# Two transformer layers with retrieved experts: all weighted v rows summed on VectorE, GpSimd left with the gathers, five row buffers instead of four

## The chip, the core and the metric

The kernel runs on one core of a Trainium2 chip. A core has TensorE (PE in the profile; its weight loads are PEld), VectorE (DVE), ScalarE (ACT), GpSimd (POOL) and SyncE (SP), each with its own instruction queue that it works off in order, and 16 DMA engines that move data between HBM and the on-chip memories. The metric is the device time of one execution in microseconds (us), as the median of several runs.

## The reference

The program is two layers of a diffusion backbone over 512 latent and 256 context tokens of width 1024. Each layer has attention (two kinds of heads, a projection before and after them, norms and gates) and then an expert retrieval, which is what the change touches:

```python
def chunk(xc):                       # 128 tokens
    q = (xc @ wq).reshape(PEER_CHUNK, PEER_HEADS, 2, PEER_DHALF)
    s = jnp.einsum('thpd,hpkd->thpk', q, sub_keys).astype(jnp.float32)
    sv, si = lax.top_k(s, PEER_TOPK)
    ...
    g = jax.nn.softmax(cv, axis=-1)
    u_sel = u[idx]                   # 128 experts for each token, rows of 1024
    v_sel = v[idx]
    a = jax.nn.gelu(jnp.einsum('td,thkd->thk', xc, u_sel).astype(jnp.float32), approximate=False)
    return jnp.einsum('thk,thkd->td', (g * a).astype(xc.dtype), v_sel)
```

Every token picks 8 x 16 = 128 of 16,384 experts. An expert is a row of u, whose product with the token gives a weight, and a row of v, which is added to the token's result with that weight. In the first layer this is done for two context tiles and four latent tiles of 128 tokens, in the second for the four latent tiles.

## The kernel before

**Two ways to the experts.** Five latent tiles (0, 1, 2 of layer 0 and 1, 2 of layer 1, `DENSE`) are *dense*: the whole table of a layer goes by once, 128 steps of 128 experts, and matrix products with all the tiles' tokens are made (`dense_experts`). Which experts count for a token is told by a weight array G, made earlier from one-hot products (`one_hots`, 32 groups of four tokens to a tile: "quads"). The five other tiles (both context tiles and latent tile 3 in layer 0, tiles 0 and 3 in layer 1) are *gathered* (`experts`): for each k of 0..127 one indirect DMA, issued by GpSimd, fetches one row per token (128 rows of 1024 float32, 512 KB) into a ring of four buffers `gv`. These five tiles are called jobs here; each has 128 u rows and then 128 v rows.

**What is done with a row.** A u row is multiplied with the tokens `btok` and summed along the row on VectorE (line 746). Of the v rows some go to VectorE, which multiplies by the token's weight and adds to accumulator 0 in one instruction (`scalar_tensor_tensor`, line 767); the others are scaled on ScalarE (line 763) and added to accumulator 1 by GpSimd (line 764). `SHARE` says who takes which by turns: half and half before the dense stream, two of three to VectorE during it. At a job's end VectorE adds the two accumulators (line 770). `LAG` = 3: the work on a row is issued behind the gather three rows later, so that rows are under way while older ones are worked on; a gather takes the buffer that the row four places earlier has left.

**Order.** Each layer begins with attention, routing, choice of experts and one-hots; there a scheduler (it simulates the program with its own idea of durations) places the instructions of each engine's queue. The gathered rows are woven in: 46% of them (353 of 768) in layer 0, 50% (256 of 512) in layer 1 (`AHEAD`). Then comes the dense stream, whose order is written by hand: a step's products and splits, and after them as many gathered rows as keep the pace even; in layer 1 only from step 16 on (`LATE`). 40 rows of layer 0 are left over for the beginning of layer 1 (`SPILL`).

**A dense step** e: the tables' tiles of step e + 1 (u) and e (v) are fetched by SP, each is split in two parts, of which ScalarE makes the leading one (line 870) and VectorE the rest (line 871); PE makes A (24 products, line 924); ScalarE applies GELU (927); VectorE multiplies by G (930); W is split as above (870, 871); PE adds the products of the step before (line 897, 18 in layer 0 and 12 in layer 1). So a step is 42 PE instructions in layer 0 and 36 in layer 1.

**One-hots.** Of the four one-hot products of a quad (`o2`), ScalarE makes one in two instructions (lines 850, 851), GpSimd one and VectorE two (line 854); VectorE also makes the other operand (842), PE multiplies (855) and ScalarE copies the result out (856).

Of the kernel before, what the change touches and what calls it, by code (L numbers as in the profile page):

```python
# [25 lines left out]
F32 = mybir.dt.float32  # L26
# [4 lines left out]
AF = mybir.ActivationFunctionType  # L31
# [3 lines left out]
D = 1024  # L35
# [15 lines left out]
# latent tiles whose experts run densely, per layer  # L51
# [6 lines left out]
ONPOOL = 1  # L58
O2B = 6
# of four tokens' one-hot products, those made on the scalar engine  # L60
ONACT = 1
ET = mybir.EngineType
MANUAL = {ET.PE, ET.DVE, ET.Activation, ET.Pool, ET.SP}
# who sums the v rows by turns: the vector engine, or the scalar engine and GpSimd
SHARE = ((0, 1), (0, 0, 1))
# rows on their way before the first is used
LAG = 3
# steps of the dense stream before it is joined by the rest of the gathered rows
LATE = (0, 16)
# gathered rows left for the next layer's beginning  # L70
SPILL = (40, 0)
# share of the gathered rows that goes ahead of the dense stream
AHEAD = (0.46, 0.5)
# float32 products of operands split exactly in two (0 the leading part), at float32 accuracy
# [5 lines left out]
# blocks of the pair list with one width: (offset, first a, number of a, width)  # L80
# [12 lines left out]
def body(ctx: ExitStack, tc: tile.TileContext, I, out):  # L93
# [6 lines left out]
    # pools of the phase at hand  # L100
# [17 lines left out]
    def gv_tile(n):  # L118
        return gat.tile([P, n], F32, tag="gv", name="gv", bufs=4)
# [14 lines left out]
    # column - row: key block before the query's may be seen where it is >= 0, the one after where <= 0  # L134
# [9 lines left out]
    # residual streams live in DRAM; hcur maps (stream, token tile) to the rows holding it now  # L144
# [23 lines left out]
    def big_w(src, cn):  # L168
        """rows of src in chunks of P, two to a tile -> [chunk] of [P, cn]."""
# [19 lines left out]
    def ada_w_early(after):  # L189
        """the same through the gather ring, which is idle before the first experts; starts once after is there."""  # L190
# [12 lines left out]
    def ada(l, m, early=None):  # L203
        """generator: appends to m the six vectors of both streams, two to a round, their four column blocks side by side."""
# [32 lines left out]
    def gate_row(t, l, i, st, n, q=nc.gpsimd):  # L237
        """t [p, 512 * x]: columns from n * 512 of gate i of the stream on every partition."""
        q.dma_start(t, gates[l, i][J[st]:J[st] + 1, n * 512:n * 512 + t.shape[1]].to_broadcast(list(t.shape)))
        return t  # L240

    def rstd_of(ss, n):
        """1 / sqrt(ss / n + eps), in place."""
# [919 lines left out]
```

## Times and profile before

| | us |
|---|---|
| runs | 4654.28, 4655.55, 4660.62 |
| median | 4655.55 |
| span of the profiled execution (first to last instruction) | 4664.8 |
| attention, routing and rows of layer 0 | 0 to 1452 |
| dense stream of layer 0 | 1452 to 2612 |
| beginning of layer 1 with 40 rows left over | 2612 to 2760 |
| attention, routing and rows of layer 1 | 2760 to 3700 |
| dense stream of layer 1 and the last rows | 3700 to 4665 |

For the profiled execution the page gives the span and no other time; it lies 9.25 us, or 0.2%, above the median of the runs. Within the stages the rows of job 0 are gathered from 348 to 1092 us, job 1 from 1104 to 1955, job 2 from 1963 to 2733, job 3 from 2970 to 3767 and job 4 from 3802 to 4638. A dense stream thus has *u stretches*, in which the rows at hand are u rows (1960 to 2345 and 3790 to 4220), and *v stretches* (1548 to 1960, 2345 to 2612, 4220 to 4640). The work of a dense step is the same in both.

### The profile page before, as it was taken

To read this page: it belongs to the slowest core of one execution; us is meant where nothing else is said; L and a number is where in the kernel's file an instruction comes from. 1 tells how busy PE (TensorE), PEld (TensorE's weight loads), DVE (VectorE), ACT (ScalarE), POOL (GpSimd) and SP (SyncE) were. 2 spreads that over 40 slices of the span, in tenths; PEclk is the share of its full clock that TensorE was granted. 3 is DMA by queue.
4 is the path that set the end of the run, shared out by engine and by line. 5 is a ranking of instruction groups with operands and counts; after the bars stand their busy time and mean duration, and the time that the engine had idled before them with its cause. 6 is when DMAs were issued, how large, how long until landed. Compare 5 with 4: busy or idle time off the path is not lost.

```text
span 4664.8 us, 59187 instructions
## 1 busy us (share of the span) xinstructions
PE 3753.1 (80%) x20350; PEld 3004.6 (64%) x20350; DVE 3507.7 (75%) x7582; ACT 1903.2 (41%) x3344; POOL 2473.8 (53%) x1818
## 2 busy tenths in 40 slices
PE   7886778597867999899999567678787688888786
PEld 2463457375756888788887445555576577776665
DVE  1256757978998888887788642767889988888887
ACT  2342334464634444333344444233465543334443
POOL 1114557685754577644466740254587744445665
PEclk9997889787988999999999889888798699999998
DMA  8578887677896988899988762788687789998887
GB/s 302 186 241 297 286 299 238 233 262 251 307 336 234 319 290 293 305 334 331 330 286 300 259 215 88 256 318 314 228 278 273 251 306 332 330 335 305 308 303 244
DMA packets 467487, 1306.55 MB, mean 280 GB/s; under 512 B 41569, under 2 KB 147809, under 8 KB 467185
## 3 DMA queue, kind: packets, MB, share of 16 engines
q0 software_dynamic: 199744, 726.26, 45.3%
q1 hardware_dynamic: 267440, 576.50, 35.5%
q8 instruction: 160, 2.62, 0.2%
q14 instruction: 143, 1.16, 0.1%
HBM read 1240.70 MB, written 61.90 MB: 279 GB/s over the span
## 4 chain that ended last, share of the span: by engine, by line
DVE 27%; issue 22%; PE 17%; DMA 16%; POOL 12%; ACT 6%; SPq 0%; POOLq 0%; ACTq 0%; DVEq 0%
POOL gv L742 9%; DMA gv<-u,idx 6%; DVE gv L746 5%; DVE vacc L767 5%; DMA gv<-v,idx 4%; POOL vacc L764 3%; PE m L632 3%; DVE v L871 3%; PE m L370 2%; ACT u L870 2%; PE m L506 2%; DVE o L854 2%; DMA raw<-uT 1%; DVE o L842 1%; DVE w L930 1%
## 5 line engine op out<-in xcount | busy, mean ns | idle before, releaser
L742 POOL DMA_INDIRECT gv<-u,idx x640 | 782.0, 1222 | 935.1 <-DVE a L746 590.8
L897 PE MATMUL o<-v,W 128*128 128x512 f32 x3840 | 973.2, 405 | 190.5 <-ACT W L870 166.4
L742 POOL DMA_INDIRECT gv<-v,idx x640 | 807.3, 1261 | 593.8 <-DVE vacc L767 318.9
L924 PE MATMUL A<-b,u 128*128 128x384 f32 (+1 forms) x6144 | 965.5, 313 | 51.5 <-ACT w L927 46.0
L924 PEld LDWEIGHTS A<-b,u 128*128 128x128 f32 x6144 | 933.2, 192 | 94.2 <-ACT w L927 73.2
L897 PEld LDWEIGHTS o<-v,W 128*128 128x128 f32 x3840 | 724.8, 193 | 379.6 <-ACT W L870 197.9
L746 DVE CUSTOM_DVE_ANT_0 gv<-gv,btok 128x1024 f32<-128x1024 f32 x640 | 766.5, 1220 | 142.7 <-DMA gv<-u,idx 141.3
L767 DVE SCALAR_TENSOR_TENSOR vacc<-gv,a,vacc 128x1024 f32<-128x1024 f32 x374 | 620.3, 1658 | 69.8 <-DMA gv<-v,idx 66.7
L764 POOL TENSOR_TENSOR vacc<-vacc,gv 128x1024 f32<-128x1024 f32 x256 | 621.6, 2428 | 79.8 <-ACT gv L763 75.6
L870 ACT ACTIVATE W<-w 128x384 fp32r<-128x384 f32 (+1 forms) x256 | 120.6, 471 | 1019.6 <-DVE w L930 1019.6
L871 DVE TENSOR_TENSOR u<-raw,u 128x1024 fp32r<-128x1024 f32 x256 | 340.8, 1331 | 131.6 <-ACT u L870 127.3
L763 ACT ACTIVATE gv<-gv,a 128x1024 f32<-128x1024 f32 x256 | 292.3, 1142 | 226.0 <-DMA gv<-v,idx 190.8
L370 PE MATMUL m<-w,aT 128*128 128x256 f32 (+3 forms) x704 | 261.1, 521 | 93.6 <-DMA w<-w_in 44.5
L871 DVE TENSOR_TENSOR W<-w,W 128x384 fp32r<-128x384 f32 (+1 forms) x256 | 208.5, 814 | 153.0 <-ACT W L870 153.0
L632 PE MATMUL m<-bT,wq 128*128 128x128 f32 x2560 | 319.4, 282 | 4.1 <-DMA wq<-wq 3.7
L871 DVE TENSOR_TENSOR v<-raw,v 128x1024 fp32r<-128x1024 f32 x256 | 313.7, 1226 | 5.5 <-ACT v L870 5.5
L632 PEld LDWEIGHTS m<-bT,wq 128*128 128x128 f32 x2560 | 306.5, 198 | 10.1 <-issue 3.7
L870 ACT ACTIVATE u<-raw 128x1024 fp32r<-128x1024 f32 x256 | 267.6, 1045 | 36.5 <-DMA raw<-uT 36.3
L370 PEld LDWEIGHTS m<-w,aT 128*128 128x128 f32 x704 | 145.7, 217 | 197.4 <-DMA w<-w_in 56.3
L870 ACT ACTIVATE v<-raw 128x1024 fp32r<-128x1024 f32 x256 | 267.4, 1045 | 7.9 <-PE o L897 7.7
L854 POOL TENSOR_SCALAR o<-io,i,gT 128x128 f32<-128x128 f32 x160 | 201.4, 1260 | 66.4 <-PE big L855 35.1
L506 PE MATMUL m<-dsu,pexp 128*128 128x128 f32 x1472 | 226.3, 299 | 6.0 <-ACT dsu L494 5.2
(215 smaller groups left out, 4923.0 us busy)
## 6 DMA issues: line engine op xcount, KB each, us to landing
raw<-uT SPq DMA_DIRECT2D x256, 512.0 KB, 5.8
raw<-v SPq DMA_DIRECT2D x256, 512.0 KB, 5.4
wq<-wq SPq DMA_DIRECT2D x144, 512.0 KB, 6.3
gv<-ada_w POOLq DMA_DIRECT2D x80, 512.0 KB, 5.6
Gd<-ar SPq DMA_DIRECT2D x80, 512.0 KB, 4.7
w<-w_out SPq DMA_DIRECT2D x72, 512.0 KB, 6.6
G<-Gd SPq DMA_DIRECT2D x16, 1536.0 KB, 13.9
G<-Gd SPq DMA_DIRECT2D x16, 1024.0 KB, 9.0
```

The source lines that it names most:

```text
L370: nc.tensor.matmul(ps[:, :cn], aT[:, k, :], w[k][:, :cn], start=(k == 0), stop=(k == KC - 1))
L506: nc.tensor.matmul(pt[:, (2 * b + x) * P:(2 * b + x + 1) * P], pe[x][0][:, (b0 + b) * P:(b0 + b + 1) * P], pe[x][1], start=True, stop=True)
L632: nc.tensor.matmul(ps[:, c], w[:, k, :], bT[:, k, :], start=(k == 0), stop=(k == KC - 1))
L742: return t, nc.gpsimd.indirect_dma_start(out=t, out_offset=None, in_=src, in_offset=bass.IndirectOffsetOnAxis(ap=idx[:, k:k + 1], axis=0))
L746: ins = nc.vector.tensor_tensor_reduce(out=t, in0=t, in1=bt, scale=1.0, scalar=0.0, op0=OP.mult, op1=OP.add, accum_out=a[:, k:k + 1])
L764: nc.gpsimd.tensor_tensor(acc, acc, t, OP.add)
L767: return nc.vector.scalar_tensor_tensor(acc, t, w[:, k:k + 1], acc, op0=OP.mult, op1=OP.add)
L854: eng.tensor_scalar(o2, io, i2[:, c], gT[:, c], op0=OP.is_equal, op1=OP.mult)
L870: nc.scalar.activation(hi, x, AF.Copy)
L871: nc.vector.tensor_tensor(lo, x, hi.bitcast(F32), OP.subtract)
L897: nc.tensor.matmul(acc[t][x], W[:, a_, c], v[:, b_, x * 512:(x + 1) * 512], start=(e == 0 and (a_, b_) == PARTS[0]), stop=(e == NK - 1 and ...
L924: nc.tensor.matmul(A, u[:, a_, k * P:(k + 1) * P], b[:, b_, k], start=(k == 0 and (a_, b_) == PARTS[0]), stop=(k == KC - 1 and (a_, b_) == ...
```

## The change

The accumulator of GpSimd is gone and with it `SHARE`: ScalarE writes the first weighted v row of a job into the one accumulator, VectorE adds the 127 others. The memory of the second accumulator (128 x 1024 float32) is a fifth buffer of the ring, and `LAG` is 4. GpSimd's one-hot product goes to ScalarE (`ONACT` 2, `ONPOOL` 0). All comments and docstrings are removed too, so lines have other numbers.

```diff
-ONPOOL = 1
+ONPOOL = 0
...
-ONACT = 1
+ONACT = 2
...
-SHARE = ((0, 1), (0, 0, 1))
...
-LAG = 3
+LAG = 4
...
-        return gat.tile([P, n], F32, tag="gv", name="gv", bufs=4)
+        return gat.tile([P, n], F32, tag="gv", name="gv", bufs=5)
...
-        def add(k, t, w, accs, begun):
-            turns = SHARE[0 if free[0] else 1]
-            x = turns[k % len(turns)]
-            if k == P - 1 and len(begun) == 1:
-                x = 1 - min(begun)
-            acc = accs[x]
-            if x not in begun:
-                begun.add(x)
-                return nc.scalar.activation(acc, t, AF.Copy, scale=w[:, k:k + 1])
-            elif x:
-                ins = nc.scalar.activation(t, t, AF.Copy, scale=w[:, k:k + 1])
-                nc.gpsimd.tensor_tensor(acc, acc, t, OP.add)
-                return ins
-            else:
-                return nc.vector.scalar_tensor_tensor(acc, t, w[:, k:k + 1], acc, op0=OP.mult, op1=OP.add)
...
+        def add(k, t, w, acc):
+            if k == 0:
+                return nc.scalar.activation(acc, t, AF.Copy, scale=w[:, 0:1])
+            return nc.vector.scalar_tensor_tensor(acc, t, w[:, k:k + 1], acc, op0=OP.mult, op1=OP.add)
...
-            accs = [gat.tile([P, D], F32, tag=f"vacc{x}", name="vacc", bufs=1) for x in range(2)]
-            begun = set()
+            acc = gat.tile([P, D], F32, tag="vacc", name="vacc", bufs=1)
```

VectorE's order in the first v stretch of layer 0's dense stream, one step, before (w, W, u and v are the step's own splits, vacc the sum of the v rows):

```order
L930 TENSOR_TENSOR w<-w,G 128x192 x2
L871 TENSOR_TENSOR W<-w,W 128x384
L871 TENSOR_TENSOR u<-raw,u 128x1024
L871 TENSOR_TENSOR v<-raw,v 128x1024
L767 SCALAR_TENSOR_TENSOR vacc<-gv,a,vacc 128x1024 x2
```

and the same step now:

```order
L914 TENSOR_TENSOR w<-w,G 128x192 x2
L855 TENSOR_TENSOR W<-w,W 128x384
L855 TENSOR_TENSOR u<-raw,u 128x1024
L855 TENSOR_TENSOR v<-raw,v 128x1024
L754 SCALAR_TENSOR_TENSOR vacc<-gv,a,vacc 128x1024 x3
```

Three v rows of a step instead of two stand in VectorE's queue; nothing else of the step has moved.

GpSimd's order from the end of job 1 to the beginning of job 2's v rows, before:

```order
L742 DMA gv<-v,idx 128x1024 x2
L802 DMA gv<-gate_91 128x1024
L764 TENSOR_TENSOR vacc<-vacc,gv 128x1024
L805 DMA gv<-h_ctx_3568 128x1024
L785 DMA btok<-b_lat_8426 128x1024
L742 DMA gv<-u,idx 128x1024 x3
L776 DMA h_ctx_10473<-gv 128x1024
L742 DMA gv<-u,idx 128x1024 x125
L742 DMA gv<-v,idx 128x1024 x9
L764 TENSOR_TENSOR vacc<-vacc,gv 128x1024
L742 DMA gv<-v,idx 128x1024 x3
L764 TENSOR_TENSOR vacc<-vacc,gv 128x1024
```

and now:

```order
L740 DMA gv<-v,idx 128x1024 x128
L786 DMA gv<-gate_91 128x1024
L789 DMA gv<-h_ctx_3568 128x1024
L770 DMA btok<-b_lat_8490 128x1024
L740 DMA gv<-u,idx 128x1024 x4
L761 DMA h_ctx_10505<-gv 128x1024
L740 DMA gv<-u,idx 128x1024 x124
L740 DMA gv<-v,idx 128x1024 x128
```

The additions that stood between the gathers are gone; GpSimd's queue holds transfers alone.

The third place is VectorE's queue in layer 0 where the one-hots of the last dense tile begin (o is the one-hot operand, mrep and i the routing of tile 3, gv and btok a gathered u row), before:

```order
L842 TENSOR_TENSOR o_8634<-io,i_8608 128x512
L830 CAST i_8612<-iy 128x128
L746 ISA gv,a<-gv,btok 128x1024
L746 ISA a 128x1
L615 MATCH_REPLACE mrep<-v_8428,m_8845 128x128
L854 TENSOR_SCALAR o_8627<-io,i_8612,gT 128x128
L854 TENSOR_SCALAR o_8630<-io,i_8612,gT 128x128
L613 MAX v_8428<-m_8845 128x8
L616 MAX v_8428<-mrep 128x8
```

and now:

```order
L826 TENSOR_TENSOR o_8699<-io,i_8672 128x512
L814 CAST i_8676<-iy 128x128
L838 TENSOR_SCALAR o_8692<-io,i_8676,gT 128x128
L838 TENSOR_SCALAR o_8695<-io,i_8676,gT 128x128
L838 TENSOR_SCALAR o_8709<-io,i_8676,gT 128x128
L838 TENSOR_SCALAR o_8712<-io,i_8676,gT 128x128
L826 TENSOR_TENSOR o_8734<-io,i_8672 128x512
L838 TENSOR_SCALAR o_8744<-io,i_8676,gT 128x128
```

The gathered rows have left this place: the scheduler has put them earlier. Counted in VectorE's whole queue, ahead of the first quad of dense tile 1 in layer 0 stood the work on 140 u rows and 63 v rows (GpSimd had 63 v rows more); now it is 221 u rows and 127 v rows. Between that quad and the dense stream stood 84 u rows and now 2. From the end of latent tile 1's attention in layer 0 to the first one-hot quad (783 to 888 us in the trace before) stood 26 rows, both engines together, now 60. In layer 1, ahead of the first quad of the last dense tile (3556 us), VectorE had 37 v rows of its job's 128 and has now 125 (up to the end of latent tile 2's attention 3 and now 21); behind that quad and ahead of the dense stream it had 15 and has none.

## Rows read from the trace of the kernel before

**Rows 1.** Part 1 of the page: busy time of each engine, its share of the span, and its instructions.

```profile
PE 3753.1 (80%) x20350; PEld 3004.6 (64%) x20350; DVE 3507.7 (75%) x7582; ACT 1903.2 (41%) x3344; POOL 2473.8 (53%) x1818
```

**Rows 2.** Busy time by stretch: start and end, length, busy us of PE, PEld, DVE, ACT, POOL (with instructions), then the granted TensorE clock as a share of full speed, the DMA engines' busy share, and GB/s.

```profile
300.00:700.00 400.00, 286.70 (x1268) 184.56 (x1266) 270.60 (x755) 129.36 (x291) 194.51 (x170) 0.81 0.83 284
700.00:1120.00 420.00, 328.04 (x1969) 254.66 (x1968) 358.22 (x1127) 204.93 (x377) 294.76 (x201) 0.84 0.72 239
1120.00:1440.00 320.00, 225.06 (x1500) 192.01 (x1499) 283.71 (x980) 152.00 (x292) 201.69 (x157) 0.81 0.84 297
...
1548.00:1960.00 412.00, 378.45 (x1857) 333.53 (x1857) 342.45 (x306) 169.84 (x219) 273.80 (x169) 0.99 0.87 298
1960.00:2345.00 385.00, 370.83 (x1848) 335.60 (x1847) 310.14 (x489) 131.45 (x181) 172.77 (x136) 0.98 0.94 331
2345.00:2612.00 267.00, 246.95 (x1206) 217.46 (x1205) 222.19 (x199) 110.26 (x143) 181.48 (x111) 0.99 0.82 283
...
3250.00:3700.00 450.00, 332.37 (x2047) 273.93 (x2046) 401.32 (x1202) 244.01 (x430) 325.04 (x232) 0.79 0.75 254
3700.00:3790.00 90.00, 77.92 (x472) 66.96 (x471) 78.13 (x81) 45.81 (x64) 51.81 (x31) 0.99 0.85 301
3790.00:4220.00 430.00, 368.33 (x2182) 322.83 (x2181) 347.46 (x569) 159.65 (x246) 174.64 (x136) 0.97 0.95 332
4220.00:4640.00 420.00, 334.84 (x1911) 279.63 (x1909) 352.19 (x344) 179.89 (x251) 265.09 (x163) 0.96 0.86 297
```

**Rows 3.** Part 5 of the page, the groups of the gathered rows: line, engine, operation, out<-in, shapes, count | busy us, mean ns of one | idle time of the engine before them and what ended most of it.

```profile
L742 POOL DMA_INDIRECT gv<-v,idx x640 | 807.3, 1261 | 593.8 <-DVE vacc L767 318.9
...
L746 DVE CUSTOM_DVE_ANT_0 gv<-gv,btok 128x1024 f32<-128x1024 f32 x640 | 766.5, 1220 | 142.7 <-DMA gv<-u,idx 141.3
L767 DVE SCALAR_TENSOR_TENSOR vacc<-gv,a,vacc 128x1024 f32<-128x1024 f32 x374 | 620.3, 1658 | 69.8 <-DMA gv<-v,idx 66.7
L764 POOL TENSOR_TENSOR vacc<-vacc,gv 128x1024 f32<-128x1024 f32 x256 | 621.6, 2428 | 79.8 <-ACT gv L763 75.6
...
L763 ACT ACTIVATE gv<-gv,a 128x1024 f32<-128x1024 f32 x256 | 292.3, 1142 | 226.0 <-DMA gv<-v,idx 190.8
```

**Rows 4.** The order of time in a v stretch of layer 0's dense stream, some lines of one step: start us, duration us (of all where several are merged, x2), engine, line, operation, and in brackets the idle time before it.

```profile
1649.33 2.42 POOL L764 TENSOR_TENSOR vacc<-vacc,gv 128x1024 f32<-128x1024 f32 x1
1649.39 3.46 DVE L871 TENSOR_TENSOR u<-raw,u 128x1024 fp32r<-128x1024 f32 x1 [0.39 <-ACT u L870]
...
1652.77 1.21 DVE L871 TENSOR_TENSOR v<-raw,v 128x1024 fp32r<-128x1024 f32 x1
...
1653.90 2.59 DVE L767 SCALAR_TENSOR_TENSOR vacc<-gv,a,vacc 128x1024 f32<-128x1024 f32 x2
```

**Rows 5.** VectorE's work in the first v stretch (1548 to 1960 us), and then in the u stretch (1960 to 2345), columns as in rows 3; ahead of them the durations of line 767 in that v stretch, in ns, as smallest/median/largest. The lines of the u stretch begin with that of line 746.

```profile
L767 DVE SCALAR_TENSOR_TENSOR vacc<-gv,a,vacc x84: 1271/1284/4055, 1559.6 to 1957.9; 128x1024 f32<-128x1024 f32 x84
...
L871 DVE TENSOR_TENSOR u<-raw,u 128x1024 fp32r<-128x1024 f32 x44 | 73.8, 1677 | 18.5 <-ACT u L870 18.5
...
L871 DVE TENSOR_TENSOR W<-w,W 128x384 fp32r<-128x384 f32 x43 | 41.4, 963 | 28.3 <-ACT W L870 28.3
...
L746 DVE CUSTOM_DVE_ANT_0 gv<-gv,btok 128x1024 f32<-128x1024 f32 x128 | 150.5, 1221 | 2.3 <-DMA gv<-u,idx 2.3
L871 DVE TENSOR_TENSOR u<-raw,u 128x1024 fp32r<-128x1024 f32 x45 | 55.1, 1225 | 29.8 <-ACT u L870 29.1 <-PE o L897 0.8
...
L871 DVE TENSOR_TENSOR W<-w,W 128x384 fp32r<-128x384 f32 x45 | 25.1, 558 | 29.3 <-ACT W L870 29.3
```

**Rows 6.** Waits over the whole span: who waited for whom, us in total, times, longest.

```profile
PEld o L897 <- ACT W L870: 197.9, 130, 17.6
ACT gv L763 <- DMA gv<-v,idx: 190.8, 71, 8.3
PE o L897 <- ACT W L870: 166.4, 118, 17.2
```

**Rows 7.** VectorE's one-hot work from 1120 to 1440 us (no additions on GpSimd there), and then from 3250 to 3700 us, columns as in rows 3.

```profile
L842 DVE TENSOR_TENSOR o<-io,i 128x512 f32<-128x512 f32 x59 | 39.9, 679 | 1.0 <-PE acc L855 0.5 <-PE big L855 0.4
L854 DVE TENSOR_SCALAR o<-io,i,gT 128x128 f32<-128x128 f32 x116 | 39.7, 377 | 7.0 <-PE acc L855 6.2 <-PE big L855 0.7
...
L854 DVE TENSOR_SCALAR o<-io,i,gT 128x128 f32<-128x128 f32 x128 | 71.6, 587 | 14.0 <-PE acc L855 9.0 <-PE big L855 4.9
...
L842 DVE TENSOR_TENSOR o<-io,i 128x512 f32<-128x512 f32 x64 | 57.2, 897 | 0.9 <-PE big L855 0.7
```

**Rows 8.** ScalarE's one-hot work over the whole span, columns as in rows 3 (160 quads, of which 96 have the form of the first line).

```profile
L856 ACT ACTIVATE ar<-acc 128x512 f32<-128x512 f32 x96 | 105.0, 1094 | 21.1 <-PE acc L855 16.8 <-DMA Gd<-ar 4.0
L851 ACT ACTIVATE o<-o,gT,nT 128x128 f32<-128x128 f32 x160 | 73.9, 465 | 0.7
...
L850 ACT ACTIVATE o<-io,i 128x128 f32<-128x128 f32 x160 | 63.3, 398 | 173.4 <-PE acc L855 84.9 <-PE big L855 68.1 <-DVE i L830 19.7
```

**Rows 9.** GpSimd's gathers from 300 to 700 us (two lines), and then its gathers and additions of the rows left over, from 2612 to 2760 us, columns as in rows 3.

```profile
L742 POOL DMA_INDIRECT gv<-u,idx x128 | 146.8, 1147 | 138.6 <-DVE a L746 83.5 <-issue 11.3 <-DVE krs L385 5.3
L742 POOL DMA_INDIRECT gv<-v,idx x21 | 23.1, 1100 | 25.7 <-ACT vacc L761 7.9 <-DVE a L746 5.6 <-DVE diag L258 4.5
...
L764 POOL TENSOR_TENSOR vacc<-vacc,gv 128x1024 f32<-128x1024 f32 x22 | 53.6, 2438 | 5.8 <-ACT gv L763 5.3
L742 POOL DMA_INDIRECT gv<-v,idx x40 | 47.2, 1179 | 20.0 <-DVE vacc L767 7.2 <-issue 6.6 <-POOL vacc L764 5.1
```

More of the change, by code (lines that the diff above doesn't have):

```diff
@@ L751, in dot, with gated, ended @@
             return ins
-        def add(k, t, w, accs, begun):
-            turns = SHARE[0 if free[0] else 1]
-            x = turns[k % len(turns)]
-            if k == P - 1 and len(begun) == 1:
-                x = 1 - min(begun)
-            acc = accs[x]
-            if x not in begun:
-                begun.add(x)
-                return nc.scalar.activation(acc, t, AF.Copy, scale=w[:, k:k + 1])
-            elif x:
-                ins = nc.scalar.activation(t, t, AF.Copy, scale=w[:, k:k + 1])
-                nc.gpsimd.tensor_tensor(acc, acc, t, OP.add)
-                return ins
-            else:
-                return nc.vector.scalar_tensor_tensor(acc, t, w[:, k:k + 1], acc, op0=OP.mult, op1=OP.add)
-        def gated(t, accs):
-            ins = nc.vector.tensor_tensor(accs[0], accs[0], accs[1], OP.add)
-            nc.vector.tensor_tensor(accs[0], accs[0], t, OP.mult)
-            return ins
-        def ended(t, accs, dst):
-            ins = nc.vector.tensor_tensor(t, t, accs[0], OP.add)
+        def add(k, t, w, acc):
+            if k == 0:
+                return nc.scalar.activation(acc, t, AF.Copy, scale=w[:, 0:1])
+            return nc.vector.scalar_tensor_tensor(acc, t, w[:, k:k + 1], acc, op0=OP.mult, op1=OP.add)
+        def gated(t, acc):
+            return nc.vector.tensor_tensor(acc, acc, t, OP.mult)
+        def ended(t, acc, dst):
+            ins = nc.vector.tensor_tensor(t, t, acc, OP.add)
             nc.gpsimd.dma_start(dst, t)
@@ L793, in experts @@
                 yield
-            accs = [gat.tile([P, D], F32, tag=f"vacc{x}", name="vacc", bufs=1) for x in range(2)]
-            begun = set()
+            acc = gat.tile([P, D], F32, tag="vacc", name="vacc", bufs=1)
             for k in range(P):
                 t, ins = gathered(I[f"v{l}"], idx, k)
-                row(partial(add, k, t, a, accs, begun), ins)
+                row(partial(add, k, t, a, acc), ins)
                 if k < P - 1:
@@ L801, in experts @@
             t = gv_tile(D)
-            row(partial(gated, t, accs), nc.gpsimd.dma_start(
+            row(partial(gated, t, acc), nc.gpsimd.dma_start(
                 t, gates[l, 5][J[st]:J[st] + 1, :].to_broadcast([P, D])))
             t = gv_tile(D)
-            row(partial(ended, t, accs, dst), nc.gpsimd.dma_start(t, hcur[st, i]))
+            row(partial(ended, t, acc, dst), nc.gpsimd.dma_start(t, hcur[st, i]))
             hcur[st, i] = dst
```

## The prediction

> **What bounds the kernel now.** I began with the busy shares: no engine is full, VectorE with 75% and PE with 80% are nearest [rows 1]. So the second view was busy time by stretch, and there it differs. In the dense streams a step is the same work throughout, and still the v stretches are slower. Counting PE's instructions, 42 to a step in layer 0, the u stretch makes 1848 / 42 = 44.0 steps in 385 us, 8.75 us each, with PE busy 371 of 385 us; the two v stretches make (1857 + 1206) / 42 = 72.9 steps in 679 us, 9.31 us each [rows 2]. In layer 1, with 36 to a step, it is 430 / 60.6 = 7.10 us against 420 / 53.1 = 7.91 us. The u stretches move 331 and 332 GB/s with the DMA engines 94 and 95% busy: they stand at PE's limit in layer 0 and at the DMA engines' in both. In the v stretches neither is full.
>
> What fills the gap shows in the order of time: GpSimd's addition starts at 1649.33 and ends at 1651.75; VectorE's split of u starts 0.06 us later and takes 3.46 us instead of the 1.2 of the split behind it, so it ends 1.1 us after the addition, which is about its own length [rows 4]. By groups, the u split takes 1677 ns on the mean in the v stretch and 1225 in the u stretch, W's 963 and 558; line 767 has a median of 1284 ns and a largest of 4055 [rows 5]. GpSimd's addition makes VectorE stand still for about its own length. The second loss is ScalarE's: it is in the queue's order behind a v row that has not come (190.8 us), and PE waits for W, which ScalarE makes behind it (166.4 us, and 197.9 for the weight loads) [rows 6].
>
> [...]
>
> **VectorE's balance.** It takes over 261 v rows (256 from GpSimd, 5 first rows from accumulators that now begin once). At the median of 1284 ns [rows 5] that is 335 us more. It gets back what the additions held up: in line 767 alone 374 x (1658 - 1284) ns = 140 us [rows 3], in the first v stretch 44 x 452 + 43 x 405 ns = 37 us of splits [rows 5], and in the one-hots of layer 1 128 x 210 + 64 x 218 ns = 41 us [rows 7]. With the other stretches it comes out about even. GpSimd loses 622 us of additions and its one-hots; ScalarE loses 256 x 1.142 = 292 us [rows 3] and takes 160 x (0.398 + 0.465) = 138 us of one-hots [rows 8].
>
> [...]
>
> **Dense streams.** A v row now costs VectorE 1.28 us and a u row 1.22 [rows 3, 5], and 2.93 rows go with a step of layer 0 ((768 - 353 - 40) / 128): a v step becomes what a u step is, with the same bytes. So the v stretches run at the u stretches' pace. Layer 0: 72.9 x (9.31 - 8.75) = 41 us; PE's idle time in the v stretches, 679 - 625.4 = 54 us, is the most there is [rows 2]; I take 48. Layer 1: 53.1 x (7.91 - 7.10) = 43 us. In the 13 steps from 3700 to 3790 us, where the last v rows of job 3 stood, PE is idle for 12 of 90 us; those rows are now done earlier, and I take 5. Together 96 us. What hides the third v row is VectorE's own slack of 75 us in the 385 of the u stretch; were a row to wait in VectorE's queue for its transfer, u, v and W behind it would wait too, and PE for them.
>
> **Rows left over, beginning of layer 1.** GpSimd's 22 additions of 2438 ns stand between its gathers: 40 rows take from 2612 to 2733 us, 3.0 us each. From 348 to 700 us, with few additions, 149 gathers take 2.36 us each [rows 9]. So the job ends 0 to 26 us earlier. The context tiles' projections don't wait for it, latent tile 3's do: I take 15.
>
> **Attention of layer 0.** The scheduler now puts the rows earlier. Where 26 rows stood in 105 us there are 60; at 2.36 us each [rows 9] these are 142 us: 37 us lost. Bounds: 0, since over the whole part to 1148 us the DMA engines moved 284 and 239 GB/s and could move 331 [rows 2]; and 130 us, if the 82 rows ahead of dense tile 1's one-hots (of 0.524 MB each) came on top at 331 GB/s. In return the stretch behind is almost free of rows: 84 dots of 1.22 us = 102 us leave VectorE, which is busy for 283.7 of 320 us there and so is the bound. Next come PE with 225 us and ScalarE with 152 + 59 x 0.863 = 203 [rows 2, 7, 8]. If PE keeps the 36 us of gaps that VectorE had, 320 becomes 261; at PE's own 225 it would be 95 less, and it may be nothing if the chain of route, choice and one-hots sets the pace. I take 55. Net: 18 us gained.
>
> **Attention of layer 1.** VectorE is full from 3250 to 3700 us (401 of 450) [rows 2]. Its job's 64 rows of GpSimd's add 82 us, and at least 41 come back from the one-hots [rows 7]. Most of these rows now stand ahead of 3556 us: there I count 15 us lost (0 to 57: 70 rows more are 90 us, less half of the 41 and 13 in line 767). Behind it 15 rows (19 us) and half of the 41 leave VectorE, 39 us; ScalarE would need 32 x (2 x 0.863 + 1.094) = 90 of 144 us [rows 8] and doesn't take over: 35 us gained. Net: 20.
>
> **The fifth buffer** lets one more gather run ahead. VectorE waits 141 us for u rows in all [rows 3], and 2.3 us in a u stretch [rows 5], so nearly all of it in attention, where it has other slack: I take 0, with at most a fifth of it, 28 us, to be had.
>
> **Sum**, against the profiled execution's span: 4664.8 - 96 - 15 - 18 - 20 = 4515.8. The page gives no other time of it; the span is 9.25 us above the median of the runs, which I take off: about 4506.
>
> **Rivals.**
> - Only the dense streams gain. Attention gives the rest back: the early rows cost 37 and 57 us, the stretches behind shrink by half of what I take (45). 4655 - 96 - 15 + 49 = 4593, between 4570 and 4640. For it: the scheduler's order knows nothing of these waits. Against it: VectorE waits for rows for 208 us in the whole span, 141 for u and 67 for v [rows 3].
> - More is gained: PE's 225 us in layer 0's attention is reached (95) without a loss before it, layer 1's last tile gains 39 and loses nothing, the dense streams 54 + 43 + 12, the rows left over 26: 269 us, 4387.
> - Slower: the gathers don't come as early as the order wants them, and VectorE, which works in order, holds attention's work behind rows that are not there. Price: 130 us in layer 0; in layer 1 88 more rows ahead of 3556 us at 331 GB/s are 139 us. With nothing back from the stretches behind, 4655 + 269 - 111 = 4813; at half the price, 4655 + 135 - 111 = 4679. It decides from 111 us on, what the dense streams and the rows left over bring. Against it: 149 rows did come at 2.36 us with four buffers.
> - The v stretches keep their pace, because VectorE waits for v rows as ScalarE did. Then 4655 - 15 - 38 = 4602 or, with attention even, 4640 to 4655. Against it: VectorE idles 2.3 us for its 128 rows in a u stretch of 385 us [rows 5], and the ring is the same.
>
> **Chances.** My forecast (4430 to 4570) 0.62, only the dense streams 0.17, more 0.08, pace kept 0.05, slower 0.08. Two runs of this kernel can't be told apart below about 0.2%, 9 us. Faster 0.89 (the first three and 0.02 of the fourth), same 0.03 (the rest of the fourth), slower 0.08. The range that holds 8 in 10 goes from 4410 to 4640.
>
> **What would show it.** In the profile after: line 767's successor 635 times with a mean near 1.28 us; the u split at 1225 ns in the v stretches too; v steps of 8.6 to 8.9 us in layer 0 and about 7.1 in layer 1; no wait of ScalarE for v rows, and PE's wait for W gone. The last one-hot tile of layer 0 should be done in 75 to 90 us and not 100, with VectorE no longer full. I am wrong if a v step stays above 9.2 us, if VectorE's idle time for v rows in attention grows beyond 100 us, or if its row operations are longer than 1.4 us without additions on GpSimd.

## The result, and the profile after

The changed kernel took 4541.1 us (median of 4 runs, 4535.4 to 4543.5) against 4658.1 us before (4654.3 to 4665.8): ratio 0.972, 95% interval 0.970 to 0.975. The forecast was 4506 with a range from 4410 to 4640; the profiled execution spans 4541.7 us where the sum gave 4515.8. One execution of e6_rows_woven below took 7648 us, far from the other three, and is left out of that kernel's figures, though not out of the 4399.7 us that a later expectation names.

The busy shares after [rows 1]:

```profile
PE 3707.9 (82%) x20350; PEld 2990.2 (66%) x20350; DVE 3376.4 (74%) x7838; ACT 1731.3 (38%) x3402; POOL 1659.9 (37%) x1402
```

VectorE has 261 row operations more and is busy for 131 us less. Why, the groups of the rows and of the splits show (line numbers are 16 smaller than before; columns as in [rows 3]):

```profile
L740 POOL DMA_INDIRECT gv<-v,idx x640 | 797.0, 1245 | 931.5 <-DVE vacc L754 593.9
L881 PE MATMUL o<-v,W 128*128 128x512 f32 x3840 | 967.3, 405 | 163.2 <-ACT W L854 161.0
...
L754 DVE SCALAR_TENSOR_TENSOR vacc<-gv,a,vacc 128x1024 f32<-128x1024 f32 x635 | 812.6, 1280 | 51.7 <-DMA gv<-v,idx 39.8
L744 DVE CUSTOM_DVE_ANT_0 gv<-gv,btok 128x1024 f32<-128x1024 f32 x640 | 764.8, 1220 | 77.8 <-DMA gv<-u,idx 75.0
...
L855 DVE TENSOR_TENSOR u<-raw,u 128x1024 fp32r<-128x1024 f32 x256 | 313.7, 1226 | 161.6 <-ACT u L854 158.9
```

The mean of a v row fell from 1658 to 1280 ns and every u split has 1226, in the v stretches too. VectorE's idle time before rows fell from 142.7 + 69.8 to 77.8 + 51.7 us. PE's wait for ScalarE's W stayed: 161.0 us where it was 166.4 [rows 6].

Busy time by stretch, columns as in [rows 2]: layer 0's last one-hots, its v, u and v stretch, the last one-hots of layer 1, and its u and v stretch:

```profile
1165.00:1420.00 255.00, 213.99 (x1529) 190.06 (x1528) 181.64 (x799) 194.69 (x427) 3.78 (x3) 0.86 0.53 179
...
1510.00:1885.00 375.00, 360.56 (x1797) 323.77 (x1796) 300.02 (x342) 121.76 (x173) 159.40 (x125) 0.99 0.92 318
1885.00:2270.00 385.00, 375.88 (x1879) 340.28 (x1878) 308.71 (x479) 129.60 (x178) 172.69 (x134) 0.99 0.94 331
...
3490.00:3610.00 120.00, 89.42 (x593) 84.71 (x594) 83.60 (x363) 89.90 (x187) 1.06 (x2) 0.76 0.51 178
...
3705.00:4090.00 385.00, 325.24 (x1937) 284.95 (x1936) 310.02 (x508) 139.47 (x215) 160.70 (x123) 0.97 0.94 332
4090.00:4515.00 425.00, 352.00 (x2058) 308.14 (x2056) 346.94 (x428) 148.27 (x229) 182.88 (x132) 0.96 0.91 316
```

By PE's instructions a v step of layer 0 now takes 375 / (1797 / 42) = 8.76 us, as a u step did before. In layer 1 it takes 425 / (2058 / 36) = 7.43 us, and a u step 7.16.

**Where the time went.** Between the starts of the same VectorE instructions in each trace (the multiplications of w that begin the second and the last step of a stream) the span falls into four parts. In us, for all kernels of this study:

| kernel | to layer 0's stream | stream 0 | to layer 1's stream | stream 1 | span |
|---|---|---|---|---|---|
| before | 1465.2 | 1145.4 | 1090.8 | 947.0 | 4664.8 |
| after | 1429.9 | 1097.0 | 1088.0 | 910.5 | 4541.7 |
| e1_stream | 1451.1 | 1092.6 | 1099.4 | 930.4 | 4589.9 |
| e2_attention | 1449.5 | 1146.6 | 1131.6 | 935.8 | 4680.1 |
| e3_onehot_on_gpsimd | 1431.3 | 1100.8 | 1068.1 | 907.6 | 4524.1 |
| e4_four_buffers | 1472.1 | 1092.5 | 1121.5 | 913.5 | 4616.0 |
| e5_memset | 1418.7 | 1078.0 | 1065.7 | 881.9 | 4460.7 |
| e6_rows_woven | 1430.7 | 1055.7 | 1085.9 | 787.4 | 4385.4 |
| e7_woven_onehot | 1430.5 | 1056.2 | 1066.8 | 792.8 | 4371.9 |
| e8_half_rows | 1432.0 | 1094.9 | 1079.6 | 860.1 | 4483.1 |
| e9_lag_3 | 1452.0 | 1099.7 | 1083.5 | 906.3 | 4557.9 |
| e10_fewer_ahead | 1411.1 | 1073.0 | 1079.4 | 794.9 | 4383.4 |

The change brought 48 us in stream 0, 37 in stream 1, 35 ahead of the first stream and 3 between the two: 123 us.

Each row is one execution, and two pairs show how firm it is. The kernel before and e1_stream have the same order on VectorE, ScalarE and GpSimd up to layer 0's stream, and still differ there by 14 us (1465.2 and 1451.1). The changed kernel and e8_half_rows have the same order up to layer 1's stream and differ by 2 us in each of the first two parts and by 8 between the streams (1088.0 and 1079.6). So in the parts ahead of the streams a difference of up to some 15 us is not told from scatter here, and the 3 us between the streams are none.

### The profile page after: what moved, and what is told of

Same layout as the page of the kernel before. It is cut to its first block, busy times and chain, and to the rows that moved or that the text cites. A ratio compares the mean times of both kernels' runs of the same rounds, so it can differ in the third digit from the quotient of the medians.

```text
span 4541.7 us, 59277 instructions
## 1 busy us (share of the span) xinstructions
PE 3707.9 (82%) x20350; PEld 2990.2 (66%) x20350; DVE 3376.4 (74%) x7838; ACT 1731.3 (38%) x3402; POOL 1659.9 (37%) x1402
## 4 chain that ended last, share of the span: by engine, by line
issue 28%; PE 26%; DVE 18%; DMA 11%; POOL 9%; ACT 6%; SPq 0%; POOLq 0%; DVEq 0%; ACTq 0%
POOL gv L740 9%; DVE vacc L754 5%; PE m L630 4%; DMA gv<-v,idx 3%; DVE gv L744 3%; PE m L504 3%; PE m L368 2%; PE A L908 2%; PE o L881 2%; DMA gv<-u,idx 2%; PE m L511 1%; DVE v L855 1%; ACT u L854 1%; DMA w<-w_in 1%; PE big L526 1%
## 5 line engine op out<-in xcount | busy, mean ns | idle before, releaser
L740 POOL DMA_INDIRECT gv<-u,idx x640 | 800.3, 1250 | 1136.5 <-DVE a L744 610.2
L740 POOL DMA_INDIRECT gv<-v,idx x640 | 797.0, 1245 | 931.5 <-DVE vacc L754 593.9
L881 PE MATMUL o<-v,W 128*128 128x512 f32 x3840 | 967.3, 405 | 163.2 <-ACT W L854 161.0
L908 PE MATMUL A<-b,u 128*128 128x384 f32 (+1 forms) x6144 | 954.9, 311 | 21.7 <-ACT w L911 18.7
L754 DVE SCALAR_TENSOR_TENSOR vacc<-gv,a,vacc 128x1024 f32<-128x1024 f32 x635 | 812.6, 1280 | 51.7 <-DMA gv<-v,idx 39.8
L744 DVE CUSTOM_DVE_ANT_0 gv<-gv,btok 128x1024 f32<-128x1024 f32 x640 | 764.8, 1220 | 77.8 <-DMA gv<-u,idx 75.0
L855 DVE TENSOR_TENSOR u<-raw,u 128x1024 fp32r<-128x1024 f32 x256 | 313.7, 1226 | 161.6 <-ACT u L854 158.9
L368 PE MATMUL m<-w,aT 128*128 128x256 f32 (+3 forms) x704 | 271.1, 536 | 105.7 <-DMA w<-w_in 55.2
L855 DVE TENSOR_TENSOR W<-w,W 128x384 fp32r<-128x384 f32 (+1 forms) x256 | 126.0, 492 | 151.0 <-ACT W L854 148.5
L504 PEld LDWEIGHTS m<-dsu,pexp 128*128 128x128 f32 x1472 | 191.8, 201 | 38.1 <-issue 23.4
L526 PE MATMUL big<-kT,qT 96*128 96x256 f32 (+1 forms) x288 | 140.7, 629 | 69.7 <-ACT pexp L485 52.3
L914 DVE TENSOR_TENSOR w<-w,G 128x192 f32<-128x192 f32 (+1 forms) x512 | 143.6, 320 | 69.9 <-DMA G<-Gd 45.7
```

Source lines behind the costliest of these rows:

```text
L368: nc.tensor.matmul(ps[:, :cn], aT[:, k, :], w[k][:, :cn], start=(k == 0), stop=(k == KC - 1))
L504: nc.tensor.matmul(pt[:, (2 * b + x) * P:(2 * b + x + 1) * P], pe[x][0][:, (b0 + b) * P:(b0 + b + 1) * P], pe[x][1], start=True, stop=True)
L526: nc.tensor.matmul(ps[:, k0:k0 + n], qT[:, h, :], kv["kT"][:, h, k0:k0 + n], start=True, stop=True)
L740: return t, nc.gpsimd.indirect_dma_start(out=t, out_offset=None, in_=src, in_offset=bass.IndirectOffsetOnAxis(ap=idx[:, k:k + 1], axis=0))
L744: ins = nc.vector.tensor_tensor_reduce(out=t, in0=t, in1=bt, scale=1.0, scalar=0.0, op0=OP.mult, op1=OP.add, accum_out=a[:, k:k + 1])
L754: return nc.vector.scalar_tensor_tensor(acc, t, w[:, k:k + 1], acc, op0=OP.mult, op1=OP.add)
```

## The experiments

My theory after the result: the collision with GpSimd's additions went, and that alone brings the streams' gain; the attention parts gain from VectorE's rows; the buffer is nothing. Rivals: the attention rows cost more than they bring, and the fifth buffer pays for them. A ratio goes to the kernel before as it ran beside each kernel; its median lay between 4658 and 4673 us, so that differences of medians between experiments carry up to 0.3% of that.

### The streams alone, and attention alone

e1_stream (the kernel before, with all v rows of the streams on VectorE):

```diff
-SHARE = ((0, 1), (0, 0, 1))
+SHARE = ((0, 1), (0,))
```

> The kernel before, with all v rows of the dense streams given to VectorE (attention's rows still shared with GpSimd, four buffers, one-hots as before). Theory: GpSimd's additions hold up VectorE, so the v stretches take the pace that they have after the change: layer 0's stream about 1097 us instead of 1145, layer 1's v stretch some 23 us shorter, about 4588 us in all. Rival (the fifth buffer and the longer lag made the streams faster): no change, 4655.

4599.8 us, ratio 0.985 (0.982 to 0.989); the span is 75 us shorter. Stream 0 gains all that the whole change gives it (1092.6 against 1097.0), without the fifth buffer and the longer lag. Stream 1 has 17 of its 37 us. The 14 us ahead of stream 0, where nothing was changed, are scatter.

e2_attention (all v rows of attention on VectorE, the streams as before):

```diff
-SHARE = ((0, 1), (0, 0, 1))
+SHARE = ((0,), (0, 0, 1))
```

> The kernel before, with all v rows of attention given to VectorE (the dense streams as before, four buffers, one-hots as before). Theory: attention of layer 0 gets shorter by about 35 us and layer 1's stays within 10 us, the first 13 steps of layer 1's stream lose some 15 us: about 4605. Rival (the early rows cost more than the stretches behind give back, and only the moved one-hots or the fifth buffer made up for it): 4655 or more.

4689.8 us, ratio 1.003 (1.001 to 1.006): no faster, if anything slower. Layer 0's attention gains 16 us, hardly more than the scatter, the part between the streams loses 41, and stream 1 gains 11 where a loss of 15 was expected: its first 32 steps take 203 us instead of 217, since the last v rows of job 3 are done before it. So taking GpSimd's additions out of attention is no gain by itself; my theory of the attention parts fell.

### The fifth buffer and the lag

e4_four_buffers (the changed kernel with the ring and the lag of before):

```diff
-LAG = 4
+LAG = 3
...
-        return gat.tile([P, n], F32, tag="gv", name="gv", bufs=5)
+        return gat.tile([P, n], F32, tag="gv", name="gv", bufs=4)
```

> The changed kernel with four row buffers and a lag of 3 again (the memory of the fifth is left unused). Theory: the fifth buffer is worth little, since rows waited mostly for VectorE: within 10 us of 4541. Rival (the fifth buffer carries the gathers of attention, and cuts VectorE's waits for rows): 20 to 50 us slower, 4560 to 4590.

4616.2 us, ratio 0.987 (0.984 to 0.991): 75 us are lost again, 42 ahead of stream 0 and 34 between the streams, none in the streams. e9_lag_3 keeps the five buffers:

```diff
-LAG = 4
+LAG = 3
```

> The changed kernel with five buffers but a lag of 3 (the work on a row stands behind the gather three places later, and one buffer is spare). Theory (attention gains from the fifth row under way, which needs the buffer and not the lag): within 10 us of 4541. Rival (the lag, by which VectorE's work meets rows that have come, brings it): 4580 to 4615, as with four buffers.

4574.3 us, ratio 0.982 (0.980 to 0.983). Of the ratios 0.972, 0.982 and 0.987 the first step is the lag's (0.009, some 42 us) and the second the buffer's (0.006, some 27); by the spans it is 16 and 58. Both count, since the three intervals lie apart; how they share stays open within that, and neither of the two sums that were expected (within 10 us of 4541, or 4580 to 4615) came. The scheduler also places attention's rows anew for each ring and lag (ahead of the first quad of layer 0 VectorE has 140 u rows in the changed kernel, 128 with four buffers, 154 with the lag of 3), so a part of each difference can be the other order. The waits of the attention of layer 0 show what both do; who waited for whom, total us, times, longest, with four buffers (300 to 1472 us):

```profile
POOL gv L740 <- DVE a L744: 142.6, 76, 22.9
DVE gv L744 <- DMA gv<-u,idx: 89.5, 74, 5.5
POOL gv L740 <- DVE vacc L754: 41.9, 23, 5.3
DVE vacc L754 <- DMA gv<-v,idx: 30.8, 25, 3.9
```

and in the changed kernel (300 to 1430 us):

```profile
POOL gv L740 <- DVE a L744: 105.2, 62, 21.3
...
POOL gv L740 <- DVE vacc L754: 35.9, 19, 5.7
...
DVE gv L744 <- DMA gv<-u,idx: 35.3, 37, 5.6
```

GpSimd waits for a buffer that a dot still reads, VectorE waits for the row behind it: a ring that is too short, seen from both ends. VectorE's 89.5 us for u rows become 35.3 (51.1 with five buffers and the lag of 3), and those 54 us are more than the 42 that this part gained. That these waits are what the buffer saves is read from the rows; no run changes them and nothing else.

### The one-hots

e3_onehot_on_gpsimd (the changed kernel with the one-hot product on GpSimd again):

```diff
-ONPOOL = 0
+ONPOOL = 1
...
-ONACT = 2
+ONACT = 1
```

> The changed kernel with the one-hot product back on GpSimd (ScalarE one, GpSimd one, VectorE two). Theory: GpSimd's one-hots (1.26 us each, 160 of them) hold up VectorE as its additions did, so layer 0's and layer 1's attention get some 10 to 30 us longer in sum: 4555 to 4570. Rival (ScalarE was the tighter one): 5 to 15 us faster, 4530.

4523.4 us, ratio 0.968 (0.965 to 0.971), 18 us below the changed kernel. That part of the change was a loss, and by the table the whole of it lies between the streams (1088.0 to 1068.1 us; e6_rows_woven and e7_woven_onehot below differ there by 19 in the same way). Ahead of stream 0 nothing was gained (1429.9 and 1431.3). In the stretches 1165:1420 and 3490:3610 above ScalarE is the busiest of VectorE, ScalarE and GpSimd (194.7 of 255 us, 89.9 of 120), while GpSimd does nothing. With the product back on GpSimd:

```profile
1180.00:1425.00 245.00, 206.63 (x1528) 184.04 (x1527) 175.55 (x768) 152.71 (x298) 78.56 (x67) 0.90 0.55 187
3490.00:3595.00 105.00, 81.99 (x592) 78.47 (x592) 74.05 (x317) 64.34 (x119) 38.82 (x34) 0.84 0.58 201
```

ScalarE's 194.7 become 152.7 us, and the last one-hot tile of each layer, from the first to the last of its quads on VectorE, takes 93 us instead of 101 and 102. In all kernels here that give VectorE all of attention's v rows, these tiles take 94 to 102 us with two products of a quad on ScalarE and 89 to 94 with one there and one on GpSimd. In layer 0 the gain seems to be lost again before: from the first quad to the 33rd, where u rows are still worked on, it takes 232 us instead of 222 (236 instead of 225 in e7_woven_onehot against e6_rows_woven), which is within the scatter. The product on GpSimd takes 1.34 us, and still it is cheaper there in the last tiles.

### Is it the collision?

e5_memset (the kernel before; GpSimd writes its accumulator instead of adding to it):

```diff
-                nc.gpsimd.tensor_tensor(acc, acc, t, OP.add)
+                nc.gpsimd.memset(acc, 0.0)
```

> The kernel before, with GpSimd's 256 additions replaced by as many memsets of accumulator 1, which read nothing (so the v rows that GpSimd would add are left out of the result). [...]

The question is whether any operation of GpSimd's holds VectorE up, so that the u split stays near its 1677 ns and W near its 963, or the additions do, so that with memsets in their place both go back to the u stretch's 1225 and 558 [rows 5].

4461.5 us, ratio 0.957 (0.955 to 0.959). VectorE's splits and GpSimd's writes from 1548 to 1860 us, in the first v stretch:

```profile
L871 DVE TENSOR_TENSOR u<-raw,u 128x1024 fp32r<-128x1024 f32 x37 | 45.3, 1225 | 22.2 <-ACT u L870 21.0 <-issue 0.8 <-PE o L897 0.4
...
L871 DVE TENSOR_TENSOR W<-w,W 128x384 fp32r<-128x384 f32 x37 | 20.6, 558 | 24.1 <-ACT W L870 23.5 <-issue 0.7
...
L764 POOL MEMSET vacc<- 128x1024 f32 x36 | 35.0, 973 | 0.0
```

Same place in the order, same size, and the u split is at 1225 ns instead of 1677, W at 558 instead of 963 [rows 5]. A memset, which only writes, does not hold VectorE up here; an addition, which reads two tiles, did. A memset is also shorter (973 against 2428 ns), but length alone is not it: 22 of the 37 u splits ran while a memset ran, and none of the 37 took more than 1.23 us, while of the 44 before the nine that ran beside an addition took 3.44 to 3.46 us each and the other 35 took 1.22 on the mean. Which property of an addition it is that does this, no run here separates. In the order of time, a split that starts 0.20 us after a memset here (the one of [rows 4] started 0.06 us after an addition and took 3.46 us):

```profile
1635.20 0.97 POOL L764 MEMSET vacc<- 128x1024 f32 x1
1635.40 1.23 DVE L871 TENSOR_TENSOR u<-raw,u 128x1024 fp32r<-128x1024 f32 x1 [0.39 <-ACT u L870]
```

The run also answers the second loss of the prediction, ScalarE standing behind v rows that have not come. Waits in layer 0's stream (who waited for whom, total us, times, longest), in the kernel before (1465 to 2611 us):

```profile
PE o L897 <- ACT W L870: 44.7, 32, 5.9
...
ACT gv L763 <- DMA gv<-v,idx: 34.1, 13, 5.2
```

and in e5_memset (1419 to 2497 us):

```profile
ACT gv L763 <- DMA gv<-v,idx: 58.7, 25, 5.1
...
PE o L897 <- ACT W L870: 8.8, 6, 2.4
```

ScalarE's wait for v rows is longer without the additions, and still PE's wait for W nearly goes and the stream is 67 us shorter: it was VectorE that made W late.

The parts ahead of the streams are 47 and 25 us shorter. That the collision costs there as well is not shown: the scheduler made another order of them, a memset takes 1.5 us less of GpSimd's time between the gathers, and it does not read the row, so that a buffer comes free sooner. What e2_attention lost thus stays unexplained in part.

### What sets a step of layer 1's stream

A v step there takes 7.43 us and not 7.10. A step in the order of time (start, duration, engine, line; in brackets the idle time before it), changed kernel:

```profile
4206.15 0.49 DVE L914 TENSOR_TENSOR w<-w,G 128x128 f32<-128x128 f32 x2
4206.73 0.42 ACT L854 ACTIVATE W<-w 128x256 fp32r<-128x256 f32 x1 [5.51 <-DVE w L914]
4207.05 1.04 ACT L854 ACTIVATE u<-raw 128x1024 fp32r<-128x1024 f32 x1
4207.17 0.43 DVE L855 TENSOR_TENSOR W<-w,W 128x256 fp32r<-128x256 f32 x1 [0.54 <-ACT W L854]
...
4207.19 4.60 PE L881 MATMUL o<-v,W 128*128 128x512 f32 x12 [2.17 <-ACT W L854]
...
4208.12 1.23 DVE L855 TENSOR_TENSOR u<-raw,u 128x1024 fp32r<-128x1024 f32 x1 [0.52 <-ACT u L854]
4208.94 0.36 ACT L911 ACTIVATE w<-A 128x256 f32<-128x256 f32 x1
4209.27 1.22 DVE L855 TENSOR_TENSOR v<-raw,v 128x1024 fp32r<-128x1024 f32 x1
...
4210.40 2.60 DVE L754 SCALAR_TENSOR_TENSOR vacc<-gv,a,vacc 128x1024 f32<-128x1024 f32 x2
...
4212.92 0.48 DVE L914 TENSOR_TENSOR w<-w,G 128x128 f32<-128x128 f32 x2
```

VectorE runs through its step without a break but for two waits for ScalarE (0.54 + 0.52 us): it has nothing to do between w and W, and ScalarE starts u only after W. The w that the chain begins with had been ready since 4209.30 and stands in VectorE's queue behind v and the rows until 4212.92; ScalarE and PE wait for it. By this step VectorE's order is the bound, and neither the DMA engines nor PE. Two runs ask this. e8_half_rows halves the rows' work in stream 1:

```diff
-            return nc.vector.scalar_tensor_tensor(acc, t, w[:, k:k + 1], acc, op0=OP.mult, op1=OP.add)
+            n = D if free[0] or len(jobs) == 3 else D // 2
+            return nc.vector.scalar_tensor_tensor(acc[:, :n], t[:, :n], w[:, k:k + 1], acc[:, :n], op0=OP.mult, op1=OP.add)
```

> The changed kernel, in layer 1's dense stream the v rows' work on VectorE cut to the first half of their width (the other half of the sum is left out; the gathers stay whole, so the bytes are the same). Theory (VectorE's order sets the v step of 7.43 us): some 2.3 rows of 0.55 us less make a v step about 6.3 to 6.8 us, and the last 64 steps take 405 to 440 us instead of 485. Rival (the DMA engines set it): 7.0 to 7.2 us, 455 us or more.

4492.7 us, ratio 0.964 (0.961 to 0.966). The last 64 steps take 434.1 us instead of 485.2, with the same bytes: VectorE sets the step and the DMA engines do not. (2.29 rows of 1.28 us, now 0.75, are 1.2 us less work in a step, and 0.8 us of it came, so VectorE's order alone does not set all of it.) e6_rows_woven keeps all work and spreads the rows of a step over three places of VectorE's order, one row between w and W, one ahead of u, the others where they stood:

```diff
         for e in range(NK):
+            yield "c"
...
-            yield
+            yield "a"
...
+            yield "b"
             W = den.tile([P, 2, T], F32R, tag="W", name="W", bufs=2)
...
-            for e, _ in enumerate(dense):
-                for _ in range(rest * max(0, e + 1 - LATE[l]) // (NK - LATE[l]) - rest * max(0, e - LATE[l]) // (NK - LATE[l])):
+            e, q, here = 0, 0, {}
+            for kind in dense:
+                if kind == "c":
+                    q = rest * max(0, e + 1 - LATE[l]) // (NK - LATE[l]) - rest * max(0, e - LATE[l]) // (NK - LATE[l])
+                    here = {"b": min(q, 1), "c": min(max(q - 1, 0), 1)}
+                    here["a"] = q - here["b"] - here["c"]
+                    e += 1
+                for _ in range(here[kind]):
```

> The changed kernel with the gathered rows of a dense step set between its splits in VectorE's order (one between w and W, one between W and u, the rest behind v) instead of all behind v. Theory (in layer 1's stream VectorE's order with its two waits for ScalarE, about 0.65 us for W and 0.65 for u, sets the step of 7.16 us in the u stretch and 7.43 in the v stretch): the waits are filled, layer 1's steps fall to 6.6 to 7.0 us and its stream gets 25 to 55 us shorter, layer 0's 0 to 20; about 4500. Rival (the DMA engines at 332 GB/s set layer 1's step): the same within 10 us.

4387.1 us (4382.9 to 4412.2), ratio 0.943 (0.939 to 0.947). Stream 1 is 123 us shorter than in the changed kernel, stream 0 41. That is far more than expected: over the 112 steps of stream 1 that have rows it is 1.1 us each, about the whole of the two waits of 0.54 and 0.52 us. A part of a step now, in the order of time:

```profile
4181.42 0.48 DVE L915 TENSOR_TENSOR w<-w,G 128x128 f32<-128x128 f32 x2
...
4181.83 1.27 DVE L754 SCALAR_TENSOR_TENSOR vacc<-gv,a,vacc 128x1024 f32<-128x1024 f32 x1
4182.00 0.42 ACT L854 ACTIVATE W<-w 128x256 fp32r<-128x256 f32 x1 [2.66 <-DVE w L915]
4182.32 1.04 ACT L854 ACTIVATE u<-raw 128x1024 fp32r<-128x1024 f32 x1
4183.02 0.41 DVE L855 TENSOR_TENSOR W<-w,W 128x256 fp32r<-128x256 f32 x1
...
4183.36 1.27 DVE L754 SCALAR_TENSOR_TENSOR vacc<-gv,a,vacc 128x1024 f32<-128x1024 f32 x1
...
4184.56 1.21 DVE L855 TENSOR_TENSOR u<-raw,u 128x1024 fp32r<-128x1024 f32 x1
```

Both waits are filled with a row, and w is multiplied sooner. By stretch (columns as in [rows 2]), in layer 0's v stretch and in layer 1's u stretch:

```profile
1510.00:1875.00 365.00, 364.04 (x1839) 330.59 (x1838) 301.54 (x351) 131.81 (x177) 168.34 (x130) 1.00 0.95 336
...
3790.00:4080.00 290.00, 266.88 (x1634) 236.57 (x1633) 259.26 (x415) 121.44 (x184) 122.55 (x103) 0.96 1.00 375
```

In layer 0 PE is busy for 364 of 365 us: here it is the limit, which it was not quite before (360.6 of 375). In layer 1 the DMA engines move 375 GB/s where I had called 332 their limit.

### Both together, and fewer rows ahead

e7_woven_onehot has the edits of e6_rows_woven and of e3_onehot_on_gpsimd.

> The changed kernel with both edits that helped alone: the rows of a dense step spread over its three places on VectorE (e6_rows_woven, 4399.7 us), and the one-hot tiles of an attention tile given to GpSimd again (e3_onehot_on_gpsimd, 17.7 us shorter than the changed kernel). Theory: the two act in different stages (the streams; the last one-hot stretches), so their gains add: 4370 to 4392 us, with the streams' lengths as in e6_rows_woven within 10 us and the last stretch of layer 1's attention near 108 instead of 119 us. Rival: with the streams on TensorE's and the DMA engines' limit, what attention saves comes back as rows that the stream has to wait for: 4395 to 4410.

4382.6 us, ratio 0.939 (0.938 to 0.941): within what the theory said. The 19 us between the streams come again (1085.9 to 1066.8), with the last stretch of layer 1's attention at 108 us, and the streams are within 6 us of e6_rows_woven; by the spans 14 us of the 18 add. The totals alone don't show it, since the two intervals overlap. The kernel takes 159 us less than the changed kernel and 284 less than the kernel before.

e10_fewer_ahead, on top of it:

```diff
-AHEAD = (0.46, 0.5)
+AHEAD = (0.42, 0.5)
```

> As e7_woven_onehot, with 13 of layer 0's 320 rows moved from attention into the stream (AHEAD 0.46 to 0.42). Theory: the first stream stands on TensorE (364.0 of 365.0 us busy in 1510:1875 of e6_rows_woven, VectorE 301.5), so rows moved into it are nearly free, and attention loses 13 x 2.5 us of VectorE's work, of which the last stretch sees a part: 10 to 30 us below e7_woven_onehot, the stream longer by under 10. Rival: VectorE's rows come back between the u and W steps and the stream grows by what attention saves: within 5 us of e7_woven_onehot, or above it.

4383.2 us, ratio 0.938 (0.936 to 0.941): no different. (The fraction is of 768 steps, a u and a v step for each row, so 31 of them moved, not 13 rows of 320.) Layer 0's attention became 19 us shorter and stream 0 17 us longer: the rival. (The part between the streams is 13 us longer in the trace, within the scatter.) The theory fell although PE is the limit of that stream in one stretch; moved rows are not free there.

## Why the prediction was right or wrong

The total was 35 us short of the median, within the range, and the direction and the likeliest case were right. Of the 35 us, 26 are the terms' and 9 the 9.25 us that I took off the span: that was the distance of one execution from its median, and for the changed kernel it is 0.6 us. The terms were not all right, and two errors hid each other, so the total came out nearer than its working deserved.

- **The collision, and stream 0**: right. Forecast 48 us, measured 48; v step forecast 8.75, measured 8.76 us; e1_stream has it alone, e5_memset without the additions and with all other work of VectorE. The second loss that I named, ScalarE behind rows that have not come, was not one (e5_memset).
- **Stream 1**: forecast 43 + 5 us, measured 37, and from other places: the 32 steps at its begin gained 15 us where I had 5, the last 64 steps 23 where I had 43. The false step is the reading that the u stretches "stand at PE's limit in layer 0 and at the DMA engines' in both", by which in layer 1, too, "a v step becomes what a u step is, with the same bytes". It became 7.43 us where a u step took 7.10 before and 7.16 after. VectorE's own order set the step, with a v row at 1.28 us, a u row at 1.22, and two waits for ScalarE in every step. e8_half_rows and e6_rows_woven show it. The sign was there in layer 0's u stretch: VectorE idle for 29.1 and 29.3 us before u and W, waiting for ScalarE [rows 5]. I counted them as slack.
- **Rows left over, 15 us**: wrong. The last of the 40 gathers was issued 40 us earlier (122 us after the stream's last w before, 82 now), but from that w to the softmax of the next tile it took 277.2 us instead of 271.1, and 269.2 in e8_half_rows with the same order as the changed kernel: no gain that shows. I had costed the job's length, and its end 40 us sooner shortened nothing.
- **Attention of layer 0, 18 us**: 35 came. The early loss was forecast near enough (37, measured 48 from the end of latent tile 1 to the first quad, and 9 more ahead of that), and so was the gain behind (55; 54 from the 33rd quad to the stream). But it came not where I said: the last one-hot tile took 101 us, not 75 to 90 (it was 100). ScalarE, with the one-hots it took over, is busy there for 80 us and VectorE for 77, and with the product back on GpSimd it is 93. The stop between it and the tile before shrank from 75 to 16 us, as the dots that stood there left. In between, from the first to the 33rd quad, 38 us came that I had not foreseen. With four buffers it is 10 us, but the kernel before and e1_stream, with the same order, differ there by 15, so how much of it is the buffer's stays open.
- **Attention of layer 1, 20 us**: 9 came at most, from the last tile's softmax to the stream (406.4 to 397.3 us), within the scatter. In e4_four_buffers the whole part between the streams is 31 us longer than before, so even this needs the buffer.
- **The fifth buffer, 0, "with at most a fifth of it, 28 us"**: the step that failed most. Measured 75 us with the lag. I took VectorE's 141 us of idle time for u rows as harmless, since it has other slack in attention. But attention is a chain of short pieces on several engines, and VectorE, in order, holds them all up while it stands at a row (89.5 us for u rows in layer 0's attention with four buffers, 35.3 with five and the longer lag); so I read the waits of e4_four_buffers above. Without the buffer the attention terms would have had the other sign (7 us lost in layer 0, 31 in layer 1): my 38 us for them and 0 for the buffer came out near the 44 measured only in sum. That is the rival "Slower: the gathers don't come as early as the order wants them", at work with a part of its price, and paid for by a term I had at nothing. That the sum came out was luck.
- **The one-hots on ScalarE**: counted inside the attention terms as free. They cost 18 us, in layer 1 alone.
- **PE's wait for W** did not go (161.0 us of 166.4). It fell from 44.7 to 20.1 us in layer 0's stream and rose from 99.9 to 122.6 in layer 1's. I had put it down to ScalarE's v rows. They are gone, and ScalarE still waits for VectorE's w, 512.6 us in layer 1's stream where it was 489.3 (waits of the changed kernel from 4040 to 4400 us, in that stream):

```profile
ACT W L854 <- DVE w L914: 218.5, 49, 7.5
...
PE o L881 <- ACT W L854: 57.0, 40, 4.2
...
DVE u L855 <- ACT u L854: 33.1, 47, 3.5
DVE W L855 <- ACT W L854: 26.1, 48, 0.5
```

In e6_rows_woven, in the same stretch of its span, the first is 158.2 us, the second 24.8, the third 4.6, and the fourth does not appear.

- **The price of a row**: right. A v row took VectorE 1.280 us on the mean where I had 1.284. GpSimd's gather of one took 1.245 us where it was 1.261 [rows 3], and that of a u row 1.250 where it was 1.222, with 261 more row operations on VectorE.

## What to carry to other kernels

Two idle times of half a microsecond before VectorE's instructions in every step (0.54 and 0.52 us) were not slack here, since it had no other break in the step; with rows in them the steps got 1.1 us shorter. So look at one step in the order of time before calling a transfer or another engine the limit, and fill such waits with work that depends on nothing near. A ring that is waited for at both ends (the producer for a buffer, the consumer for its data) may be worth a buffer: here that and a longer lag brought 75 us. When GpSimd is freed, try giving back what little it can do where another engine is busier: here it helped in the last one-hot tiles (93 us instead of 101 and 102), and brought nothing to layer 0 as a whole.

## What was not expected of the hardware

The DMA engines were 95% busy at 332 GB/s before, and 100% busy at 375 GB/s in e6_rows_woven: the same kinds of transfers, 13% more bytes for 5% more busy share. A busy share near full was no measure of the bytes that could still go.

Ahead of any gather the kernels with five buffers are slower: their first gather starts at 354 to 361 us, with four at 347 to 348. The transfers of the first weights go through the same ring; whether that is why was not tried. Nor was a sixth buffer.
